# Second group of seven block products in units 1 to 7 of a SwiGLU, chains begun in five stages, gate2's modulation in the last product

## The chip, the cores and the metric

The kernel runs on one core of one Trainium2 chip. The metric is the device time of one launch in microseconds. The core's engines work side by side, each in the order of its own queue: TensorE (PE in the profile, its weight loads PEld) multiplies, VectorE (DVE) and ScalarE (ACT) do elementwise work, GpSimd (POOL) hardly anything here, and SP issues the DMA transfers.

## The reference

One layer of a decoder trunk on 256 tokens with 2048 channels, all in float32. The change touches the end of the first sub-layer's output projection (w_out) and the second sub-layer, a SwiGLU with 5632 hidden channels:

```python
mod = jax.nn.silu(c) @ w_ada[l] + b_ada[l]
shift1, scale1, gate1, shift2, scale2, gate2 = jnp.split(mod[:, None, :], N_MOD, axis=-1)
...
x = x + gate1 * mixing_sublayer(h, ...)          # ends in y @ w_out
h = rms_norm(x, norm2_gain[l]) * (1 + scale2) + shift2
gate, up = jnp.split(h @ w_ffn_in[l], 2, axis=-1)
x = x + gate2 * ((silu(gate) * up) @ w_ffn_out[l])
```

## The kernel before, in words

**Products.** The 256 tokens are two tiles of 128; the weights are the moving operand, in blocks of 512 columns, and the contraction goes in chunks of 128 rows. Each float32 operand is split into a high part that TensorE takes as it is and a low rest, and a product is three matmuls (`mm3`, L199 to L201): high times high, high times low, low times high. A chunk of a block is thus 2 x 3 matmuls of 128x512. The split of the weights goes by pairs of chunks, 128x1024: a DMA into a raw room (`raw_tile`, 512 KB), a cast on ScalarE that makes the high half (L189), a subtraction on VectorE that makes the low half (L196, in `halve`). The halves have four rooms (`whi`, `wlo`); a few pairs get tiles of their own (`spare`, `front`). The raw rooms are a list (`free_rooms`) that loads take from at the front and give back to at the end; `more_rooms` and `fewer_rooms` add tiles to it and take them out.

**Units.** The gate and up products of the SwiGLU go in 11 units of 512 hidden channels: unit i has gate block i (`pg`) and up block NFF + i (`pu`), 16 chunks each. Unit 0 is plain. From unit 1 on the first four chunks of the two blocks are a 2x2 by 2x2 block product (two token tiles, two column blocks, two pairs of chunks) done with seven block products instead of eight: `paired`. Its left sides are sums of pieces of the activations, made once (`left_sums`); its right sides are the weights' raw pieces `b11`, `b12`, `b21`, `b22` and differences of them (`t1`, `t2`, `t3` and one more), made on VectorE in `differ` into the tiles named in `places`, and each of the seven is cast and split. A product is of one token tile, so a pair of halves serves 6 matmuls there instead of 12. In the middle an intermediate sum is moved between banks (copies on ScalarE; `add` on VectorE, L1376). `paired` is a generator: the caller runs a piece of it between pieces of the up block of the unit before, so that its chain begins before it is needed. The last product (w_ffn_out, 44 chunks, four column blocks taken in two pairs) uses `paired` with two such groups (eight chunks).

The silu of the gate (L1418) and the product with the up block (L1440) give the activation, whose transposes and splits (L221, L222) are put off in `later` to a place within the following block.

**Order.** The order on each engine is fixed when the program is written out, by a scheduler that takes by priority what its own model of the engines has ready; `prio` moves a piece forward, `tc.issue_after(ins)` puts one behind `ins` on its engine. From the end of unit 0 on (`state["ordered"]`) all subtractions and differences of the weights stand on VectorE in the order in which they are written.

**gate2.** The modulation vectors are sums over 16 row blocks of w_ada, weighted by silu(c): background work (`bg`), one step per call of `tick`, which `block` calls once per pair of chunks with `state["rate"]` steps. A gate2 step is a DMA of 512 KB into a tile of the ring `ring["tags"]` and a multiply-add on VectorE (L318), 32 in all. What follows (`after`) is `rows_of`: the bias is added, and in eight rounds the sum is cast (L976), its rest taken (L977) and multiplied by ones on TensorE (L981, L982), which adds the partitions and spreads the row; each quarter is copied back (L983). One tile, T6, serves all rounds. `flush` runs what is left. Before the change gate2 goes on in units 0 to 10, and `add_out` (L1459 multiply, L1461 add) puts out each column block of the last product right after it is done.

**w_out.** The last column block of w_out has all its weights loaded ahead; the normalisation that follows and the first unit's loads are placed around it by hand (`order`, which names for each pair of chunks of unit 0 what its cast and its subtraction stand behind).

Of the kernel before, what the change touches and what calls it, by code (L numbers as in the profile page):

```python
# [17 lines left out]
P = 128  # L18
T = 256
NT = T // P  # L20
D = 2048
KC = D // P
DFF = 5632
NB = 512
# [5 lines left out]
N_DIL = 6  # L30
N_GLA = 4
SEG_SHIFT1, SEG_SCALE1, SEG_GATE1, SEG_SHIFT2, SEG_SCALE2, SEG_GATE2 = range(6)
RATE_IN, RATE_MID, RATE_FFN = 0.8, 0.6, 0.4
DEFER = 4
AHEAD = 4000
WARM = (22, 43, 10, 3)
# [4 lines left out]
NFF = 11  # L41
# [26 lines left out]
def trunk(ctx: ExitStack, tc: tile.TileContext, I, out):  # L68
# [117 lines left out]

    def halve(hi, lo, raw, high_behind=None, low_behind=None):
        with behind_it(high_behind):
            nc.scalar.copy(hi, raw)  # L189
# [1092 lines left out]
    KF = 4 * NFF  # L1282
    w_fo = I["w_ffn_out"]
    PLACES = [("A13", "A14"), ("A2", "A3")]
    LATE = {8: ("KC", "AR0"), 9: ("AR1", "A15")}

    def left_sums(tags, scratch, xh, xl):

# [9 lines left out]
        nc.vector.tensor_tensor(lo, raw, hi.bitcast(F32), op=ALU.subtract)  # L1298
        return hi, lo

    def paired(act, sums, places, src, b0, b1, k1):

        n = len(places)
        p0 = c11, c21 = [acc_bank() for _ in range(NT)]

        def halved(raw):
            hi, lo = halves_room()
# [12 lines left out]
            for r in raws:  # L1320
                give_back(r)

        with prio():
            b11, b12 = load(0, b0), load(0, b1)
            first = [halved(r) for r in b11]

        def times(ps, left, right, g, start=False):
            hi, lo = right
            for i in range(2):
# [6 lines left out]

        total = lambda q: lambda g, i: (sums[g][0][:, q, i, :], sums[g][1][:, q, i, :])
        part = lambda c, t: lambda g, i: act(4 * g + c + i, t)
        product(c11, part(0, 0), True)
# [42 lines left out]
        add(c22)  # L1382
        for q, (w, right) in enumerate(rest):
            k = 4 * n + 2 * q
            block(p0, act, None, k, k + 2, 0, w=w, go_on=True, more=True, seeded=True)
# [4 lines left out]
        block(p0, act, src, 8 * n, k1, b0, go_on=True, seeded=True)  # L1390
        yield p0, p1

    for i in range(NFF):
        if i == 0:
            pg = [acc_bank() for _ in range(NT)]
            one = turns[0]
            order = {2: (one["root"], one["spread"]), 3: (one["root"], one["spread"]), 4: (one["rows"], one["low"][0]),
                     5: (one["high"][0], one["low"][0]), 6: (one["high"][1], one["low"][1]), 7: (one["high"][2], one["low"][2])}
            w = load_weights(
                w_ff, 0, KC, 0, front=("A12", "KD", "AR0", "AR1"), spare=("A9", "A10", "A0", "A1"), behind=order  # L1400
            )
            for t in range(NT):
                block(pg, h2_at, None, 0, KC, 0, w=w, tiles=(t,), steps=steps if t == 0 else {})
            bg.append(gate2_bg())
            pu = [acc_bank() for _ in range(NT)]
        else:
            state["rate"] = (2 if i < 7 else 4) * RATE_FFN
            pg, pu = next(work)
            state["rate"] = 0.0
            if i in LATE:  # L1410
                assert not macs
                with prio():
                    act_sums.append(left_sums(LATE[i], ("A13", "A14"), *act[i - min(LATE)]))
        sgs = []
        with prio():
            for t in range(NT):
                sg = scr([P, NB])
                nc.scalar.activation(sg, pg[t], AF.Silu)  # L1418
                sgs.append(sg)
        if i == 0:  # L1420
            block(pu, h2_at, w_ff, 0, KC - 4, NFF, more=True)
            h2_sums = [left_sums(("A2", "A3"), ("A13", "A14"), h2[0][0], h2[1][0])]
            fewer_rooms("KC")
            more_rooms("A4", "A8")
            state["ordered"] = True
        else:
            block(pu, h2_at, w_ff, 4, KC - 4, NFF + i, go_on=True, more=True, seeded=True)
        if i < NFF - 1:
            work = paired(h2_at, h2_sums, [("A13", "A14")], w_ff, i + 1, NFF + i + 1, KC)
        else:  # L1430
            work = paired(act_at, act_sums, PLACES, w_fo, 0, 1, KF)
        next(work)
        block(pu, h2_at, w_ff, KC - 4, KC - 2, NFF + i, go_on=True, more=True, seeded=i > 0)
        next(work)
        block(pu, h2_at, w_ff, KC - 2, KC, NFF + i, go_on=True, seeded=i > 0)
# [12 lines left out]
    x2 = []  # L1448
    for n in range(4):
        xr = S(f"H{4 + n}", [P, NT, NB])  # L1450
        nc.sync.dma_start(xr, x2_far[:, n])
        x2.append(xr)

    LASTK, LASTC = 4, NB // 2

# [8 lines left out]

    CUT = KF - 14
    K0 = 4 * len(act_sums)
    for n in range(4):
        if n % 2 == 0:
            both = next(work)
        pss = both[n % 2]  # L1470
        if n == 3:
            fewer_rooms("H2", "H3")
            block(pss, act_at, w_fo, K0, CUT, n, more=True, go_on=True, seeded=True)
            w = load_weights(w_fo, CUT, KF, n, spare=("H2", "H3", "H4", "H5", "A2", "A3"))
# [15 lines left out]
        else:  # L1490
            if n == 1:
                block(pss, act_at, w_fo, K0, KF - 10, n, go_on=True, more=True, seeded=True)
                more_rooms("H2", "H3")
                work = paired(act_at, act_sums, PLACES, w_fo, 2, 3, KF)
                next(work)
                block(pss, act_at, w_fo, KF - 10, KF - 6, n, go_on=True, more=True, seeded=True)
                next(work)
                block(pss, act_at, w_fo, KF - 6, KF, n, go_on=True, seeded=True)
            if n == 0:
                flush()  # L1500
                gate2 = state["gate2"]
                with prio():
                    for t in range(NT):
                        add_out(n, t, pss[t])
                continue
            kept = S("H4", [P, NT, NB])
            with prio():
                for t in range(NT):
                    nc.scalar.copy(kept[:, t, :], pss[t])
            for t in range(NT):  # L1510
                add_out(n, t, kept[:, t, :])
# [47 lines left out]
```

## Time and profile before

| | |
|---|---|
| median of 3 runs | 1613.75 us (1612.1 to 1616.0) |
| the profiled execution's own time | 1612.38 us |
| its span, first to last instruction | 1610.6 us, mean granted clock 0.998 |
| DMA | 399.24 MB, mean 248 GB/s |
| units 2 to 6 | 43.5 to 43.6 us each |
| last product, 1363.62 to the last tail | 241.65 us |

The rows below are of four kinds. A row of a timeline has the start in us, the duration, the engine, the line, the operation, out<-in, the shape and in brackets how long the engine sat idle before it and what ended that. A matmul's duration is modelled and overlaps its successor's start, so two starts are compared, not the durations. A row of groups has the busy time and the mean in ns, then the idle time ahead of it. A row of windows has for each engine busy us and the number of operations, then TensorE's granted clock, the DMA engines' busy share and GB/s. A buffer's number is left out of its name: A is any of A0 to A15.

### The profile page before, as it was taken

Reading aid. Unit: us, or ns where it says so; the run is one execution under the profiler, and the core shown is the slowest. Engines: PE = TensorE matmul, PEld = TensorE weight load, DVE = VectorE, ACT = ScalarE, POOL = GpSimd, SP = SyncE. Lnnn points to the kernel's source line nnn. Section 1 sums busy time; section 2 is a strip of 40 time slices with the busy share of each in tenths; the row PEclk is TensorE's granted clock in tenths of the full one; section 3 lists DMA queues with packets and bytes.
Section 4 is the critical chain, followed back from the end, with each engine's and each line's share of the span. In section 5 each row is a group of like instructions: output and inputs, shape, how many; then the busy total and the mean of one; then the engine's idle time right before and its main releaser. Section 6 shows DMA issues by size and latency. Waiting matters only on the chain.

```text
span 1610.6 us, 20073 instructions
## 1 busy us (share of the span) xinstructions
PE 1590.7 (99%) x7273; PEld 1307.7 (81%) x7273; DVE 1241.9 (77%) x1420; ACT 851.7 (53%) x1183; POOL 5.3 (0%) x14
## 2 busy tenths in 40 slices
PE   9999999999999999999999999999999999999999
PEld 7878888788888888888887788888888888787887
DVE  6889995887888787878757788888888776856753
ACT  5654449755576444444445555555555555534542
POOL 1000000000000000000000000000000000000000
PEclk9999999999999999999999999999999999999999
DMA  9999997884776889888677577777776567765662
GB/s 335 346 330 322 330 313 222 279 264 143 253 237 217 308 301 319 309 292 310 211 210 240 176 251 259 233 247 253 246 240 191 175 194 225 260 204 177 229 179 86
DMA packets 116179, 399.24 MB, mean 248 GB/s; under 512 B 13090, under 2 KB 13896, under 8 KB 116080
## 3 DMA queue, kind: packets, MB, share of 16 engines
q1 hardware_dynamic: 115856, 397.95, 74.0%
q8 instruction: 57, 0.93, 0.2%
q14 instruction: 42, 0.34, 0.1%
q0 software_dynamic: 224, 0.01, 0.0%
HBM read 393.71 MB, written 4.19 MB: 247 GB/s over the span
## 4 chain that ended last, share of the span: by engine, by line
PE 87%; DVE 6%; issue 2%; ACT 2%; DMA 2%; ACTq 0%; DVEq 0%; SPq 0%
PE acc L201 26%; PE acc L200 26%; PE acc L199 26%; DVE wlo L196 3%; PE acc L461 1%; ACT whi L189 1%; DMA AR<-ada_rest 1%; PE misc L1104 1%; DVE ada L318 1%; PE misc L201 1%; DVE A L196 1%; PE misc L817 1%; PE misc L199 1%; PE misc L200 1%; DVE scr L1440 0%
## 5 line engine op out<-in xcount | busy, mean ns | idle before, releaser
L189 ACT CAST whi<-raw 128x1024 fp32r<-128x1024 f32 (+1 forms) x447 | 457.9, 1028 | 484.2 <-PE acc L201 364.2
L196 DVE TENSOR_TENSOR wlo<-raw,whi 128x1024 fp32r<-128x1024 f32 (+1 forms) x447 | 528.8, 1191 | 230.7 <-ACT whi L189 228.0
L200 PE MATMUL acc<-wlo,H 128*128 128x512 f32 x1476 | 576.8, 391 | 1.1 <-DVE wlo L196 1.0
L201 PE MATMUL acc<-whi,H 128*128 128x512 f32 x1476 | 576.8, 391 | 0.4 <-DVE H L480 0.4
L199 PE MATMUL acc<-whi,H 128*128 128x512 f32 x1476 | 576.4, 391 | 0.4 <-ACT H L473 0.4
L201 PEld LDWEIGHTS acc<-whi,H 128*128 128x128 f32 x1476 | 277.0, 188 | 59.0 <-DVE H L480 1.8
L200 PEld LDWEIGHTS acc<-wlo,H 128*128 128x128 f32 x1476 | 277.2, 188 | 58.0 <-DVE wlo L196 2.2
L199 PEld LDWEIGHTS acc<-whi,H 128*128 128x128 f32 x1476 | 277.1, 188 | 57.4 <-ACT H L473 1.3
L196 DVE TENSOR_TENSOR wlo<-A,whi 128x1024 fp32r<-128x1024 f32 x133 | 161.1, 1222 | 69.7 <-ACT whi L189 68.6
L189 ACT CAST whi<-A 128x1024 fp32r<-128x1024 f32 x133 | 139.8, 1053 | 131.1 <-PE acc L201 92.7
L199 PE MATMUL acc<-whi,A 128*128 128x512 f32 x332 | 130.5, 395 | 2.5 <-DVE acc L1376 1.6
L200 PE MATMUL acc<-wlo,A 128*128 128x512 f32 x332 | 129.6, 390 | 0.2 <-DVE wlo L196 0.2
L201 PE MATMUL acc<-whi,A 128*128 128x512 f32 x312 | 121.6, 390 | 0.0
L318 DVE SCALAR_TENSOR_TENSOR ada<-AR,csil,ada 128x1024 f32<-128x1024 f32 x59 | 75.1, 1279 | 6.3 <-DMA AR<-ada_rest 6.3
L199 PEld LDWEIGHTS acc<-whi,A 128*128 128x128 f32 x332 | 62.3, 188 | 19.6 <-DVE acc L1376 5.8
L200 PEld LDWEIGHTS acc<-wlo,A 128*128 128x128 f32 x332 | 62.4, 188 | 13.3 <-DVE wlo L196 0.9
L201 PEld LDWEIGHTS acc<-whi,A 128*128 128x128 f32 x312 | 58.6, 188 | 12.4
L199 PE MATMUL acc<-whi,T 128*128 128x512 f32 x120 | 46.8, 390 | 0.0
L201 PE MATMUL acc<-whi,T 128*128 128x512 f32 x120 | 46.7, 389 | 0.0
L200 PE MATMUL acc<-wlo,T 128*128 128x512 f32 x120 | 46.7, 389 | 0.0
L201 PE MATMUL acc<-whi,OS 128*128 128x512 f32 x112 | 43.6, 389 | 0.0
L517 ACT COPY A<-acc 128x512 f32<-128x512 f32 x50 | 29.0, 586 | 15.9 <-PE acc L201 14.6
(404 smaller groups left out, 1499.9 us busy)
## 6 DMA issues: line engine op xcount, KB each, us to landing
raw<-w_in SPq DMA_DIRECT2D x203, 512.0 KB, 4.9
raw<-w_ffn_in SPq DMA_DIRECT2D x122, 512.0 KB, 4.5
AR<-ada_rest SPq DMA_DIRECT2D x79, 512.0 KB, 5.0
raw<-w_ffn_out SPq DMA_DIRECT2D x53, 512.0 KB, 3.9
A<-w_ffn_in SPq DMA_DIRECT2D x52, 512.0 KB, 3.9
raw<-w_out SPq DMA_DIRECT2D x32, 512.0 KB, 3.8
KC<-ada_rest SPq DMA_DIRECT2D x30, 512.0 KB, 4.7
A<-w_ffn_out SPq DMA_DIRECT2D x29, 512.0 KB, 4.5
```

The costliest lines, as they stand in the source:

```text
L189: nc.scalar.copy(hi, raw)
L196: return nc.vector.tensor_tensor(*args, **kw)
L199: nc.tensor.matmul(ps, lh, rh, start=start, stop=False, skip_group_check=seeded)
L200: nc.tensor.matmul(ps, lh, rl, start=False, stop=False, skip_group_check=seeded)
L201: state["mm"] = nc.tensor.matmul(ps, ll, rh, start=False, stop=stop, skip_group_check=seeded)
L318: nc.vector.scalar_tensor_tensor(acc, raw, c, acc, op0=ALU.mult, op1=ALU.add)
L461: state["warm"] = nc.tensor.matmul(ps, ones_r, wide, start=True, stop=True)
L517: nc.scalar.copy(A[b][:, t, :], pss[t])
L817: nc.tensor.matmul(ps[:n, t * N_GLA + h, :].rearrange("p (s l) -> p s l", l=L), at(f, h, t)[:, :n], odd(at(f, h, t)), start=True, stop=True,)
L1104: nc.tensor.transpose(ps[:, i, :], src[:, i * P : (i + 1) * P], ident)
```

## The change

Unit i has `pairs_of(i)` groups: two in units 1 to 7, one in units 8 to 10 as before. A second set of left sums of the normalised activations is made after unit 0's gate block, in AR0, AR1. `paired` yields five times: loads and the first differences; the first product; the second product; the third difference; the rest. With `early` the differences `t2` come in the first piece. `with_stages` runs these pieces between pieces of the up block, or of the second column block in the last product. The raw rooms get OD, KD, OS1, OS2 as well until units 7 and 8. gate2's steps leave the units for the last product (ring H2, H3, H5, rate 0.65, then 2.6 for its rows); the first three column blocks of the result are kept (`keep`) and put out at the end, after `flush` at chunk 30 of the fourth, when x2 is read back too. The w_out loads of the last block are written after `flush` and `more_rooms("KC")`, and unit 0's first two casts and subtractions stand behind w_out's last (`cast3`, `split3`).

```diff
-RATE_IN, RATE_MID, RATE_FFN = 0.8, 0.6, 0.4
+RATE_IN, RATE_MID, RATE_OUT, RATE_ROWS = 0.8, 0.6, 0.65, 2.6
...
-    w = load_weights(I["w_out"], 0, KC, 3, spare=("T0", "T3", "OS0", "OS1", "OS2", "OD", "A7", "A11"))
     flush()
     more_rooms("KC")
+    w = load_weights(I["w_out"], 0, KC, 3, spare=("T0", "T3", "OS0", "OS1", "OS2", "OD", "A7", "A11"))
+    cast3, split3 = state["cast"], state["split"]
...
-    state["rate"] = RATE_FFN
-    ring["tags"] = ("AR0", "AR1", "KC")
+    state["rate"] = 0.0
...
     PLACES = [("A13", "A14"), ("A2", "A3")]
-    LATE = {8: ("KC", "AR0"), 9: ("AR1", "A15")}
+    UNIT_PLACES = [("A13", "A14"), ("KC", "A15")]
+    LATE = {9: (("KC", "AR0"), ("AR1", "A15")), 10: (("AR1", "A15"), ("A13", "A14"))}
+
+    def pairs_of(i):
+        return 2 if i < 8 else 1
...
-    def paired(act, sums, places, src, b0, b1, k1):
+    def paired(act, sums, places, src, b0, b1, k1, early):
...
+        def second_differences():
+            b22 = load(2, b1)
+            return b22, [differ(y, t, p[1]) for p, y, t in zip(places, b22, t1)]
+
+        with prio():
+            b11, b12 = load(0, b0), load(0, b1)
+            t1 = [differ(y, x, p[0]) for p, x, y in zip(places, b11, b12)]
+            if early:
+                b22, t2 = second_differences()
+        yield
+        p0 = c11, c21 = [acc_bank() for _ in range(NT)]
+        with prio():
+            first += [halved(r) for r in b11]
+            all_back(b11)
         product(c11, part(0, 0), True)
...
         yield
         side, held = misc_bank([P, NB]), scr([P, NB])
         with prio():
-            t1 = [differ(y, x, p[0]) for p, x, y in zip(places, b11, b12)]
-            all_back(b11)
             first += [halved(t) for t in t1]
-            b22 = load(2, b1)
-            t2 = [differ(y, t, p[1]) for p, y, t in zip(places, b22, t1)]
-            t3 = [differ(y, x, p[0]) for p, x, y in zip(places, b12, b22)]
-            all_back(b12)
+            if not early:
+                b22, t2 = second_differences()
         product(side, total(0), True)
...
+        yield
+        with prio():
+            t3 = [differ(y, x, p[0]) for p, x, y in zip(places, b12, b22)]
+            all_back(b12)
         yield
...
+    def in_pieces(pss, act, src, k0, k1, b, more=False):
+
+        for k in range(k0, k1, 6):
+            end = min(k + 6, k1)
+            block(pss, act, src, k, end, b, go_on=True, more=more or end < k1, seeded=True)
+            if not bg:
+                state["rate"] = RATE_ROWS
+
+    def with_stages(work, pss, act, src, k0, cuts, b):
+
+        k = k0
+        for cut in cuts:
+            if cut > k:
+                block(pss, act, src, k, cut, b, go_on=k > 0, more=cut < cuts[-1], seeded=k0 > 0)
+                k = cut
+            if cut < cuts[-1]:
+                next(work)
...
-            order = {2: (one["root"], one["spread"]), ...
+            order = {0: (cast3, split3), 1: (cast3, split3), 2: (one["root"], one["spread"]), ...
...
-            bg.append(gate2_bg())
...
         if i == 0:
-            block(pu, h2_at, w_ff, 0, KC - 4, NFF, more=True)
+            fewer_rooms("KC")
             h2_sums = [left_sums(("A2", "A3"), ("A13", "A14"), h2[0][0], h2[1][0])]
-            fewer_rooms("KC")
-            more_rooms("A4", "A8")
+            h2_sums.append(left_sums(("AR0", "AR1"), ("KC", "A15"), h2[0][1], h2[1][1]))
+            more_rooms("A4", "A8", "OD", "KD", "OS1", "OS2")
             state["ordered"] = True
+        if i in (7, 8):
+            fewer_rooms(*(("OS1", "OS2") if i == 7 else ("OD", "KD")))
+        if i < NFF - 1:
+            work = paired(h2_at, h2_sums, UNIT_PLACES[: pairs_of(i + 1)], w_ff, i + 1, NFF + i + 1, KC, True)
+            cuts = (KC - 8, KC - 4, KC - 2, KC - 2, KC)
         else:
...
+            work = paired(act_at, act_sums, PLACES, w_fo, 0, 1, KF, False)
+            cuts = (KC - 8, KC - 8, KC - 4, KC - 2, KC)
+        with_stages(work, pu, h2_at, w_ff, 0 if i == 0 else 4 * pairs_of(i), cuts, NFF + i)
...
+    ring["tags"] = ("H2", "H3", "H5")
+    bg.append(gate2_bg())
+    state["rate"] = RATE_OUT
     for n in range(4):
...
         if n == 3:
...
+            in_pieces(pss, act_at, w_fo, K0, CUT, n, more=True)
+            state["rate"] = 0.0
+            flush()
+            gate2 = state["gate2"]
+            for m, tag in ((0, "H4"), (1, "H2"), (2, "H3"), (3, "H5")):
+                x2_back(m, tag)
+            w = load_weights(w_fo, CUT, KF, n, spare=("A13", "A14", "KC", "AR0", "A2", "A3"))
+            for m in range(n):
+                for t in range(NT):
+                    add_out(m, t, kept[m][:, t, :])
...
+        if n == 1:
+            in_pieces(pss, act_at, w_fo, K0, KF - 14, n, more=True)
+            rate, state["rate"] = state["rate"], 0.0
+            work = paired(act_at, act_sums, PLACES, w_fo, 2, 3, KF, False)
+            with_stages(work, pss, act_at, w_fo, KF - 14, (KF - 12, KF - 10, KF - 6, KF - 4, KF), n)
+            state["rate"] = rate
+        keep(n, ("H6", "H7", "AR1")[n])
```

More of the change, by code (lines that the diff above doesn't have):

```diff
@@ L188, in halve @@
         with behind_it(high_behind):
-            nc.scalar.copy(hi, raw)
+            state["cast"] = nc.scalar.copy(hi, raw)
         with behind_it(low_behind):
@@ L1321, in all_back @@
                 give_back(r)
-        with prio():
-            b11, b12 = load(0, b0), load(0, b1)
-            first = [halved(r) for r in b11]
         def times(ps, left, right, g, start=False):
@@ L1338, in paired @@
         part = lambda c, t: lambda g, i: act(4 * g + c + i, t)
+        first = []
+        def second_differences():
[11 more added lines that the diff above has]
+            all_back(b11)
         product(c11, part(0, 0), True)
@@ L1384, in paired @@
             k = 4 * n + 2 * q
-            block(p0, act, None, k, k + 2, 0, w=w, go_on=True, more=True, seeded=True)
+            if q == 2 and later:
+                with tc.issue_after(state["mm"].ins), prio():
+                    later.pop()()
+            block(p0, act, None, k, k + 2, 0, w=w, go_on=True, more=k + 2 < k1, seeded=True)
+            if not bg:
+                state["rate"] = RATE_ROWS
             if q < n:
@@ L1389, in paired @@
                 times(c21, part(2, 1), right, q - n)
-        block(p0, act, src, 8 * n, k1, b0, go_on=True, seeded=True)
+        in_pieces(p0, act, src, 8 * n, k1, b0)
         yield p0, p1
+    def in_pieces(pss, act, src, k0, k1, b, more=False):
+        for k in range(k0, k1, 6):
+            end = min(k + 6, k1)
+            block(pss, act, src, k, end, b, go_on=True, more=more or end < k1, seeded=True)
+            if not bg:
+                state["rate"] = RATE_ROWS
+    def with_stages(work, pss, act, src, k0, cuts, b):
[6 more added lines that the diff above has]
+                next(work)
     for i in range(NFF):
@@ L1396, in trunk @@
             one = turns[0]
-            order = {2: (one["root"], one["spread"]), 3: (one["root"], one["spread"]), 4: (one["rows"], one["low"][0]),
+            order = {0: (cast3, split3), 1: (cast3, split3), 2: (one["root"], one["spread"]), 3: (one["root"], one["spread"]), 4: (one["rows"], one["low"][0]),
                      5: (one["high"][0], one["low"][0]), 6: (one["high"][1], one["low"][1]), 7: (one["high"][2], one["low"][2])}
@@ L1447, in trunk, with x2_back, keep @@
         act.append((hi, lo))
[L1448 to L1452, printed above, removed]
+    x2, kept = {}, {}
+    def x2_back(n, tag):
+        x2[n] = S(tag, [P, NT, NB])
+        nc.sync.dma_start(x2[n], x2_far[:, n])
+    def keep(n, tag):
+        kept[n] = S(tag, [P, NT, NB])
+        with prio():
+            for t in range(NT):
+                nc.scalar.copy(kept[n][:, t, :], both[n % 2][t])
     LASTK, LASTC = 4, NB // 2
@@ L1471, in trunk @@
         if n == 3:
-            fewer_rooms("H2", "H3")
-            block(pss, act_at, w_fo, K0, CUT, n, more=True, go_on=True, seeded=True)
-            w = load_weights(w_fo, CUT, KF, n, spare=("H2", "H3", "H4", "H5", "A2", "A3"))
+            in_pieces(pss, act_at, w_fo, K0, CUT, n, more=True)
[6 more added lines that the diff above has]
+            for m in range(n):
+                for t in range(NT):
+                    add_out(m, t, kept[m][:, t, :])
             block(pss, act_at, None, CUT, KF, 0, w=w, tiles=(0,), go_on=True, seeded=True)
@@ L1489, in trunk @@
             add_out(n, 1, side, NB - LASTC, base=NB - LASTC)
[L1490 to L1511, printed above, removed]
+            continue
+        if n == 1:
[5 more added lines that the diff above has]
+        keep(n, ("H6", "H7", "AR1")[n])
 _INS = ["x", "c", "b_ada", "norm1_gain", "norm2_gain", "sb_q_gain", "sb_k_gain", "dil_q_gain", "dil_k_gain", "w_gla_a",
```

15 lines of the change are left out of this document (1 added, 14 removed).

## The prediction, on record before the result

> **What bounds the kernel now.** I read the page's parts 1, 4 and 5 first, then cut the FFN stage into windows at the same cast of each unit, then read TensorE's rows in order of time wherever two starts lay further apart than usual. The page gives TensorE 99% of the span and the chain that ended last 87% of it; the windows name busy time and operations of TensorE, its weight loads, VectorE, ScalarE and GpSimd, then clock, DMA share and GB/s.
>
> ```profile
> PE 1590.7 (99%) x7273; PEld 1307.7 (81%) x7273; DVE 1241.9 (77%) x1420; ACT 851.7 (53%) x1183; POOL 5.3 (0%) x14
> PE 87%; DVE 6%; issue 2%; ACT 2%; DMA 2%; ACTq 0%; DVEq 0%; SPq 0%
> ```
> ```profile
> 896.00:930.53 34.53, 34.52 (x145) 27.81 (x144) 25.03 (x31) 20.26 (x26) 0.00 (x0) 0.96 0.54 168
> 1061.17:1104.73 43.56, 43.40 (x195) 35.67 (x194) 36.51 (x35) 22.94 (x26) 0.00 (x0) 1.00 0.74 254
> 1363.62:1605.27 241.65, 239.38 (x1063) 197.24 (x1062) 148.91 (x136) 108.73 (x109) 0.00 (x0) 1.00 0.62 195
> ```
>
> A unit takes 43.56 us. A busy share proves little, so look at the starts (timeline of TensorE, one unit):
>
> ```profile
> 1049.84 0.39 PE L200 MATMUL acc<-wlo,H 128*128 128x512 f32 x1
> ...
> 1058.90 0.39 PE L201 MATMUL acc<-whi,H 128*128 128x512 f32 x1
> ...
> 1065.93 0.39 PE L199 MATMUL acc<-whi,H 128*128 128x512 f32 x1
> 1066.48 0.50 PE L199 MATMUL acc<-whi,A 128*128 128x512 f32 x1 [0.16 <-DVE acc L1376]
> ```
>
> The first two rows lie 40 matmuls apart: 9.06/40 = 0.2265 us each, without a hole. The last two hold the unit's only stall, 0.55 - 0.2265 = 0.32 us, while VectorE adds a finished product into the next bank. So TensorE issues all the time, and a matmul that is left out is worth its 0.2265 us unless another engine falls behind.
>
> **The products.** Four 128-row chunks of two column blocks cost 4 x 2 x 2 x 3 = 48 matmuls plainly and 7 x 2 x 3 = 42 as a group. Units 1 to 7 get a second group: 6 fewer in each, 42 in all, 42 x 0.2265 = 9.5 us less. Units 8 to 10 and the last product keep their counts.
>
> The Trainium skill ("TensorE: Matmul & The Clock Gate", Back-to-back issue gap) gives N/2.4 + 2.5 ns, 216 ns at N = 512, for an isolated gap; by that the 42 would bring an estimated 9.1 us. The same section gives 131 ns for a sustained stream, by which they would bring 5.5 us and the case would end near 1608. The spacing here lies above both, over 40 intervals in a row, which leaves the second no chance.
>
> **Ordering of the w_out casts.** Timeline of TensorE, and of ScalarE:
>
> ```profile
> 865.57 0.39 PE L201 MATMUL acc<-OS,A 128*128 128x512 f32 x1
> 866.45 0.49 PE L199 MATMUL acc<-A,A 128*128 128x512 f32 x1 [0.49 <-ACT A L189]
> 867.71 0.50 PE L200 MATMUL acc<-A,A 128*128 128x512 f32 x1 [0.76 <-DVE A L196]
> 862.82 1.05 ACT L189 CAST A<-raw 128x1024 fp32r<-128x1024 f32 x1 [2.66 <-DMA raw<-w_ffn_in]
> 865.34 1.06 ACT L189 CAST A<-raw 128x1024 fp32r<-128x1024 f32 x1
> ```
>
> ScalarE sits 2.66 us for a piece of w_ffn_in with the last pair of w_out cast only behind it; TensorE loses 2.14 - 2 x 0.2265 = 1.7 us. The change puts the first two w_ffn_in casts behind w_out's (cast3, split3) and lends w_out the room KC. The moved halves are needed only behind w_out's second token tile, 48 matmuls or 10.9 us later, so no matmul waits anew; behind the two casts on ScalarE stand the norm's squares, which wait for w_out's end in any case: -1.7 us, or 0 if the norm chain behind it binds instead.
>
> **What pays for it.** A group needs seven halved right sides where four did: three more casts on ScalarE and three more subtractions on VectorE, and four differences. The gate2 sums (L318) leave the units. Groups of one unit, 1061.17 to 1104.73, and two rows of VectorE's timeline, 1.14 us apart at 1.22 us each:
>
> ```profile
> L318 DVE SCALAR_TENSOR_TENSOR ada<-AR,csil,ada 128x1024 f32<-128x1024 f32 x4 | 5.0, 1278 | 0.0
> L318 DVE SCALAR_TENSOR_TENSOR ada<-KC,csil,ada 128x1024 f32<-128x1024 f32 x1 | 1.3, 1279 | 0.0
> 1058.03 1.22 DVE L196 TENSOR_TENSOR wlo<-raw,whi 128x1024 fp32r<-128x1024 f32 x1
> 1059.17 1.22 DVE L196 TENSOR_TENSOR wlo<-A,whi 128x1024 fp32r<-128x1024 f32 x1
> ```
>
> VectorE per unit: 36.5 - 6.3 (five sums) + 7 x 1.14 = 38.2 us. TensorE: 43.56 - 1.36 = 42.2. ScalarE: 22.9 + 3 x 1.05 = 26.1, with the cast of the rows above. So on average all fits, VectorE at 90%. Two things decide locally. The halves have four rooms, so ScalarE's cast waits until TensorE has used the fourth one back; and subtractions and differences run strictly in the written order. In the new order the four early differences of the next unit (t1, t2) stand between the last subtraction of the paired stage and the first weights of the up block. Counted from the third of the four mixed steps there: the last room frees as that step begins, and its half is ready some 2.6 us in (cast 1.05, subtraction 1.22, waits), then come four differences, 4.6, the transposed activation's two subtractions of half the size, 1.2, and the up block's subtraction, 1.1: 9.5 us. TensorE comes for it after 36 matmuls, 8.2, and the eight transposes (43.56 - 186 x 0.2265 - 0.32 leaves 1.1 for them), and needs the low half one matmul later: 9.5. So nothing is spare there; the other halves come out early by 0.6 us or more. The old stall of 0.32 goes, since the product that covers the add is twice as long (12 matmuls, 2.7 us). What comes instead is a wait for wlo at the up block. Bounds per unit: 0, and 1.43, which is what the first front of two groups in this trace costs today (next part). I take 0.3, the old size, so the units bring 9.5 us, with ends of 7 x (1.36 + 0.32) = 11.8 and 11.8 - 7 x 1.43 = 1.8.
>
> **The two transitions into the paired last product.** Each front today is written in one piece:
>
> ```profile
> 1371.19 0.39 PE L199 MATMUL acc<-whi,KC 128*128 128x512 f32 x1
> 1372.52 0.50 PE L199 MATMUL acc<-whi,A 128*128 128x512 f32 x1 [0.94 <-ACT whi L189]
> 1383.13 0.39 PE L199 MATMUL acc<-whi,KC 128*128 128x512 f32 x1
> 1383.68 0.50 PE L200 MATMUL acc<-wlo,A 128*128 128x512 f32 x1 [0.16 <-DVE wlo L196]
> ...
> 1484.95 0.61 PE L199 MATMUL acc<-whi,OD 128*128 128x512 f32 x2
> 1486.73 0.50 PE L199 MATMUL acc<-whi,KC 128*128 128x512 f32 x1 [1.17 <-ACT whi L189]
> ```
>
> The first costs 1.33 + 0.55 less two intervals, 1.43 us, the second 1.78 less two (its first row holds two matmuls), 1.33 us, 2.8 in all. Spread over five stages most of it should go: -1.9 us, between -2.8 and 0.
>
> **Unit 0.** Here lies the first front of two groups. Its window (896.00 to 930.53) has 34.5 - 25.0 = 9.5 us of VectorE idle. Added are the second set of left sums, two subtractions and three differences (5 x 1.14 = 5.7). The sums' rows:
>
> ```profile
> 895.97 1.22 DVE L1291 TENSOR_TENSOR A<-H,H 128x1024 f32<-128x1024 f32 x1
> ...
> 898.31 0.42 DVE L1293 TENSOR_TENSOR A<-A 128x256 f32<-128x256 f32 x1
> ```
>
> One sum of 1.22, four of 0.42 and a last subtraction as large as the first make 4.1 us, so 9.8 us against 9.5. I take +1.5 us, from 0 to 4.
>
> **gate2 in the last product.** The 32 sums, 32 x 1.28 = 41 us of VectorE, go at 0.65 per pair of chunks into a stretch (1363.62 to 1605.27) with 241.7 - 148.9 = 92.7 us of VectorE idle, and 32 x 0.52 MB over some 150 us (49 pairs of chunks and the front between) add 112 GB/s to its 195, about 307, where the first unit row above shows 254 at a DMA share of 0.74. I cost both at nothing; that slack hides them, and with it gone each sum would cost its 1.28. The rest is at the end. By the rates the sums end in the last column block near chunk 20, the rows' turning is written at chunk 30, and its ones-products stand behind that chunk's matmul: 84 matmuls, 19.0 us, before TensorE's end. Eight rounds of cast, subtraction and two products follow each other through one buffer, T6. One such round:
>
> ```profile
> 1303.17 0.60 ACT L983 COPY ada<-misc 128x512 f32<-128x512 f32 x1
> 1303.65 0.43 ACT L976 CAST T<-ada 128x256 fp32r<-128x256 f32 x1
> 1305.90 0.40 ACT L976 CAST T<-ada 128x256 fp32r<-128x256 f32 x1
> 1597.04 0.69 DVE L1459 TENSOR_TENSOR scr<-ada,acc 128x512 f32<-128x512 f32 x1 [3.80 <-PE acc L201]
> 1605.27 0.75 DVE L1459 TENSOR_TENSOR scr<-ada,acc 128x256 f32<-128x256 f32 x2 [6.82 <-PE acc L201]
> ```
>
> From 1303.65 to 1305.90, 2.25 us a round, 0.48 more where a quarter is copied. Seven rounds and three copies: 17.2 us, the last products and copy take an estimated 2.0 more (the round without its cast and subtraction, and 0.60): 19.2, so the fourth quarter is there 0.2 us past TensorE's end. Today its first tile is modulated at 1597.04, nine us before the end, and the tail starts at 1605.27. Then that tile's multiply and add (2 x 0.69) push the tail back by about 2.8 us; three earlier blocks' multiplies (12 x 0.69) get in the rounds' way for some 0.5. I take +3.3 us. Low end 0 (rounds without other work in between), high end 8. On SP's queue the four reloads of x2 (2 MB) move from the stage's start to chunk 30 and six stores of 256 KB wait with their adds: 3.6 MB in 19 us, 190 GB/s, where no weights are left to load; costed at nothing, else at the one or two us that the last store would queue.
>
> **Sum.** -9.5 - 1.7 - 1.9 + 1.5 + 3.3 = -8.3 us. The profiled execution took 1612.4 us (span 1610.6), 1.4 under the median 1613.75: 1612.4 - 8.3 = 1604.1, said as 1604.
>
> **The rivals.**
> Fronts as today's: each unit's front stalls the 1.43 us of the first transition and the transitions stay as they are. Then the units bring 1.8 us, and the sum is -1.8 - 1.7 + 1.5 + 3.3 = +1.3: 1614, no change. For it: that front has the same two groups. Against it: it had six raw rooms, here ten, and six differences in a row. Chance 0.09.
>
> Slower: the lateness at the up block grows past 2 us and the clock falls with it. Its rows:
>
> ```profile
> 892.64 0.39 PE L201 MATMUL acc<-A,H 128*128 128x512 f32 x1
> 894.75 0.50 PE L199 MATMUL acc<-A,H 128*128 128x512 f32 x1 [1.72 <-ACT H L1214]
> ...
> 898.46 0.63 PE L199 MATMUL acc<-AR,H 128*128 128x512 f32 x1
> 898.89 0.49 PE L200 MATMUL acc<-AR,H 128*128 128x512 f32 x1
> ```
>
> After a hole of 1.9 us, matmuls start 0.43 apart instead of 0.2265 for some ten, 2.0 us more; the holes of 1.1 and 1.3 us above had no such sequel. Per unit 1.9 + 2.0 - 0.32 - 1.36 = +2.2, seven units +15.5, with the other terms (+1.2) 1629. It decides from about 1.8 us of lateness a unit; my working gives none. Chance 0.07.
> The Trainium skill (the same page, Part 1: The HAM clock gate) halves the clock only after an idle window of about 3.4 us; by that, holes of 1.9 us would cost themselves alone and this case would end near 1615. The trace shows half speed after a shorter hole.
>
> A late end: the rounds take 3.4 us as other work gets between; 7 x 1.15 = 8 us later, 1612 or a little less, on the edge of no change. Chance 0.07. Better than forecast (no stall in units 0 to 7, both transitions clean, the tail hidden): 11.8 + 1.7 + 2.8 = 16.3 less, 1596. Chance 0.10.
>
> **How the numbers follow.** The forecast (1598 to 1609, its bounds partly summed) has 0.67, better 0.10, as today's 0.09, late end 0.07, slower 0.07. The range 1596 to 1610 leaves out the no-change case, the slower one and a small part of the late end and of the better one, 0.2 in all. A change of 0.2%, 3.2 us, is about what this measurement can tell: faster 0.80 (half of the late end with it), same 0.13, slower 0.07.
>
> **What would show it.** TensorE 42 matmuls fewer, units 1 to 7 at 42.2 us, spacing 0.2265, VectorE 38 us busy in each; no wait at the old L1376 add but one for wlo at the up block; no ScalarE wait for w_ffn_in ahead of the last w_out cast; transitions with holes under 0.6 us each; from chunk 30 of the last block eight rounds of L976 and the first tile's multiply only after TensorE's end. I am wrong if a unit takes over 43, if DMA waits appear in the last product, or if the end lies over 8 us behind TensorE's last matmul.

## The result, and the profile after

The changed kernel takes 1597.88 us in the median (1595.6 to 1599.4, 4 runs) against 1613.8 us before: 15.9 us less, a ratio of 0.990 [0.988, 0.992]. The forecast was 1604 with a range from 1596 to 1610. The direction and its reason held; the gain was nearly twice the 8.3 us that the terms had made, and the time lies near the low end of the range.

The page of the changed kernel, part 1, and three windows as before (a unit, from its transposes to the next unit's; unit 0; the last product up to 1570):

```profile
PE 1579.5 (99%) x7231; PEld 1299.8 (81%) x7231; DVE 1298.4 (81%) x1475; ACT 877.0 (55%) x1207; POOL 5.3 (0%) x14
898.00:933.50 35.50, 35.49 (x148) 28.29 (x148) 31.85 (x39) 21.58 (x27) 0.00 (x0) 0.96 0.48 154
1079.13:1120.98 41.85, 41.85 (x190) 34.47 (x189) 38.28 (x37) 26.23 (x28) 0.00 (x0) 1.00 0.60 203
1377.90:1570.00 192.10, 192.10 (x849) 158.99 (x848) 144.60 (x128) 89.47 (x92) 0.00 (x0) 1.00 0.83 286
```

TensorE has 42 matmuls fewer, and where the windows of before had a gap between their length and TensorE's busy time, these have none: a unit is 41.85 us long and TensorE is busy for 41.85. VectorE's 38.28 us are what the prediction had added up.

The holes can be read off the waits of TensorE's matmuls, from 905 us to the end, of before and of after:

```profile
PE acc L199 <- ACT whi L189: 2.1, 2, 1.2
PE acc L199 <- DVE acc L1376: 1.6, 10, 0.2
PE acc L200 <- DVE wlo L196: 0.2, 1, 0.2
```
```profile
PE acc L199 <- DVE acc L1391: 0.5, 3, 0.2
```

The add into the next bank was waited for in ten units and is now in three, those that kept one group. Two spans cannot be compared straight, though. The chain of work shows one and the same piece, the transposes of w_out's third block, in the kernel before and in the changed one:

```profile
838.30 0.87 PE misc L1170 x8
```
```profile
841.80 0.87 PE misc L1170 x8
```

The changed kernel's profile is 3.5 us late there, and by chance: two more profiles of the changed kernel (e0 and e10 below) have TensorE begin these transposes at 838.64 and 838.35 us, where these two have 838.13 and 841.63. From there on the two take 1610.6 - 838.3 = 772.3 and 1597.2 - 841.8 = 755.4 us: the profiles differ by 16.9 us in what the change touches.

Three places that both profiles have tell where these 16.9 us lie: TensorE's first matmul behind the normalisation (at 894.75 before and 896.39 after), its wait for the add in unit 8, which has one group in both, and its last matmul (at 1606.39 and 1593.03). The half speed that the last section tells of follows the first of these places in both. The wait in unit 8, before and after:

```profile
1240.69 0.50 PE L199 MATMUL acc<-whi,A 128*128 128x512 f32 x1 [0.16 <-DVE acc L1376]
```
```profile
1230.54 0.50 PE L199 MATMUL acc<-whi,A 128*128 128x512 f32 x1 [0.16 <-DVE acc L1391]
```

Up to the normalisation the changed kernel is 1.9 us shorter, from there to unit 8 11.8 us (345.9 and 334.2), from unit 8 to the last matmul 3.2 us (365.7 and 362.5), and behind the last matmul both take 4.2 us.

### The profile page after: what moved, and what is told of

It is laid out like the page before. It is cut to its first block, busy times and chain, and to the rows that moved or that the text cites. A ratio compares the mean times of both kernels' runs of the same rounds, so it can differ in the third digit from the quotient of the medians.

```text
span 1597.2 us, 20101 instructions
## 1 busy us (share of the span) xinstructions
PE 1579.5 (99%) x7231; PEld 1299.8 (81%) x7231; DVE 1298.4 (81%) x1475; ACT 877.0 (55%) x1207; POOL 5.3 (0%) x14
## 4 chain that ended last, share of the span: by engine, by line
PE 92%; DVE 4%; DMA 2%; issue 1%; ACT 1%; POOL 0%; ACTq 0%; DVEq 0%; POOLq 0%; SPq 0%
PE acc L201 28%; PE acc L199 28%; PE acc L200 28%; DVE wlo L196 1%; DMA AR<-ada_rest 1%; PE misc L201 1%; PE misc L200 1%; PE misc L199 1%; PE misc L1104 1%; PE acc L461 1%; DVE ada L318 1%; PE misc L817 1%; ACT whi L189 1%; PE misc L454 0%; DMA H<-c 0%
## 5 line engine op out<-in xcount | busy, mean ns | idle before, releaser
L189 ACT CAST whi<-raw 128x1024 fp32r<-128x1024 f32 (+1 forms) x424 | 433.6, 1026 | 454.9 <-PE acc L201 340.2
L196 DVE TENSOR_TENSOR wlo<-raw,whi 128x1024 fp32r<-128x1024 f32 (+1 forms) x424 | 500.7, 1190 | 189.8 <-ACT whi L189 188.2
L200 PE MATMUL acc<-wlo,H 128*128 128x512 f32 x1406 | 550.7, 392 | 1.1 <-DVE wlo L196 1.0
L201 PE MATMUL acc<-whi,H 128*128 128x512 f32 x1406 | 550.7, 392 | 0.4 <-DVE H L480 0.4
L199 PE MATMUL acc<-whi,H 128*128 128x512 f32 x1406 | 549.5, 392 | 0.4 <-ACT H L473 0.4
L200 PEld LDWEIGHTS acc<-wlo,H 128*128 128x128 f32 x1406 | 264.6, 188 | 56.7 <-DVE wlo L196 3.5
L201 PEld LDWEIGHTS acc<-whi,H 128*128 128x128 f32 x1406 | 264.3, 188 | 56.2 <-DVE H L480 1.8
L199 PEld LDWEIGHTS acc<-whi,H 128*128 128x128 f32 x1406 | 264.5, 188 | 55.8 <-DVE acc L1391 1.3
L318 DVE SCALAR_TENSOR_TENSOR ada<-AR,csil,ada 128x1024 f32<-128x1024 f32 x39 | 49.7, 1280 | 7.7 <-DMA AR<-ada_rest 7.7
L318 DVE SCALAR_TENSOR_TENSOR ada<-H,csil,ada 128x1024 f32<-128x1024 f32 x30 | 37.5, 1279 | 0.1
```

What stands on the lines that cost most here:

```text
L189: state["cast"] = nc.scalar.copy(hi, raw)
L196: return nc.vector.tensor_tensor(*args, **kw)
L199: nc.tensor.matmul(ps, lh, rh, start=start, stop=False, skip_group_check=seeded)
L200: nc.tensor.matmul(ps, lh, rl, start=False, stop=False, skip_group_check=seeded)
L201: state["mm"] = nc.tensor.matmul(ps, ll, rh, start=False, stop=stop, skip_group_check=seeded)
L318: nc.vector.scalar_tensor_tensor(acc, raw, c, acc, op0=ALU.mult, op1=ALU.add)
```

## The experiments

Each ratio is to the kernel before, with its interval; each kernel is the changed one with one edit.

### The changed kernel as a reference, twice

> The changed kernel itself, so that the variants have it on the same chip. Both theories: about 16 us under the kernel before (1597.9 against 1613.8), units 1 to 7 of 41.8 us without a hole on TensorE.

> The changed kernel once more, beside the next one: 1596 to 1598.

Measured 1596.5 us, 0.990 [0.989, 0.991], and 1596.1 us, 0.990 [0.989, 0.991].

### One group in units 1 to 7

```diff
-        return 2 if i < 8 else 1
+        return 1
```

> All as in the changed kernel, but one group of block products in units 1 to 7. Theory A (TensorE's issue sets the time; what is gained is matmuls and holes): the 42 matmuls come back (+9.5) and with them the hole at the add into the next bank, 7 x 0.32 to 0.44 (+2.2 to 3.1): 1609 to 1611, units of 43.5 us. Rival B (the units got faster because gate2's sums and loads left VectorE and the DMA queues): most of the gain stays, 1598 to 1602, units of 42 us or so.

Measured 1607.9 us, 0.997 [0.996, 0.998]: 11.4 us over the changed kernel. A unit (window, from transposes to transposes):

```profile
1020.40:1063.97 43.57, 43.41 (x196) 35.66 (x195) 31.04 (x30) 22.94 (x25) 0.00 (x0) 1.00 0.60 193
```

The unit is 43.57 us long as before the change, though VectorE is busy for 31.0 us instead of 36.5 and the DMA moves 193 GB/s instead of 254. So a VectorE and DMA queues relieved of gate2 bring the units nothing by themselves; rival B falls. The group is worth 42 x 0.2265 + 7 x 0.32 = 11.8 us by the rows of before, and 11.4 was measured. From the first matmul behind the normalisation to unit 8's add this run's profile takes 346.0 us, against 334.2 in the changed kernel's: 11.8.

### Fronts in two pieces, and only the second differences late

```diff
-  ... w_ff, i + 1, NFF + i + 1, KC, True)
-            cuts = (KC - 8, KC - 4, KC - 2, KC - 2, KC)
+  ... w_ff, i + 1, NFF + i + 1, KC, False)
+            cuts = (KC - 4, KC - 4, KC - 2, KC - 2, KC)      # not in the second run
```

> The fronts of units 1 to 10 written in two pieces, as before the change, with the second differences late; groups, rooms and gate2 as in the changed kernel. If the five stages carry the two groups: holes at each front as at the first transition of the kernel before, 1.4 us in units 1 to 7, so about +10 us, 1608. If the ten raw rooms and the free VectorE are enough by themselves: units of 41.8 to 42.2 us, 1598 to 1601.

> The five stages as in the changed kernel, but the second differences of units 1 to 10 in the third stage instead of the first. The fronts in two pieces cost a hole of 0.88 us in each of seven units. If the place of the second differences makes it: the same holes, +6 us, 1602 to 1603. If the stages make it: no holes, 1597. If both do: holes of about 0.4 us, 1599 to 1600.

Measured 1602.6 us, 0.993 [0.992, 0.995], with two pieces, and 1604.9 us, 0.995 [0.994, 0.996], with five stages and the second differences late. TensorE at the front of the fourth unit, two pieces first, then five stages:

```profile
1064.04 0.39 PE L199 MATMUL acc<-whi,A 128*128 128x512 f32 x1
1065.03 0.50 PE L200 MATMUL acc<-wlo,H 128*128 128x512 f32 x1 [0.60 <-DVE wlo L196]
```
```profile
1062.28 0.39 PE L199 MATMUL acc<-whi,A 128*128 128x512 f32 x1
1063.27 0.50 PE L200 MATMUL acc<-wlo,H 128*128 128x512 f32 x1 [0.60 <-DVE wlo L196]
```

The same hole to a hundredth, 0.99 - 0.2265 = 0.76 us and a slow start behind it, in each of seven units. VectorE's rows just ahead of it, in the run with five stages:

```profile
1057.46 1.22 DVE L196 TENSOR_TENSOR A<-A,A 128x1024 f32<-128x1024 f32 x1
1058.59 1.22 DVE L196 TENSOR_TENSOR A<-raw,KC 128x1024 f32<-128x1024 f32 x1
1059.73 1.22 DVE L196 TENSOR_TENSOR A<-A,raw 128x1024 f32<-128x1024 f32 x1
1060.86 1.22 DVE L196 TENSOR_TENSOR KC<-raw,A 128x1024 f32<-128x1024 f32 x1
1062.00 1.22 DVE L196 TENSOR_TENSOR wlo<-raw,whi 128x1024 fp32r<-128x1024 f32 x1
```

Four differences in a row stand ahead of the low half that TensorE waits for; it comes at 1062.00 + 1.22 and the matmul starts at 1063.27. That the pieces are spread over five stages does not matter as long as those four lie there. What carries the two groups is that the second differences lie in the first piece, before the up block's weights, and by the times that is worth 6 to 9 us, or 0.9 to 1.3 a unit; by the traces it is 1.0 a unit, as the next front lies 42.84 us behind the one shown in both runs, where a unit of the changed kernel takes 41.85. Whether two pieces would do with the second differences early was not run, nor what the four added raw rooms are worth. Here the waits of the changed kernel's weight loads, units 1 to 7:

```profile
PEld acc L199 <- DVE acc L1391: 1.3, 7, 0.2
PEld acc L200 <- DVE wlo L196: 1.1, 6, 0.2
```

Both waits are still there, in seven and in six of the seven units, 0.2 us long, and TensorE's matmuls show none of it there. The front fits with little to spare.

### gate2 back in the units

```diff
-    state["rate"] = 0.0
+    state["rate"] = 0.7
+    ring["tags"] = ("T3", "T4", "T5")
...
+            bg.append(gate2_bg())             # after unit 0's gate block
...
-    ring["tags"] = ("H2", "H3", "H5")
-    bg.append(gate2_bg())
```

> gate2's 32 sums back in units 0 to 6 (ring T3, T4, T5, rate 0.7), nothing of it in the last product; two groups as in the changed kernel. If VectorE's room decides: 38.3 us busy plus 5.5 sums of 1.19 us make 44.8 us against TensorE's 41.8, so these units go to 44 to 45 us, +13 to +19 us in six or seven units, 1611 to 1616. If VectorE's idle time can take them (its 38.3 us hold waits that the sums could fill only in part): units of 42 to 43 us, 1599 to 1605. If gate2 in the units cost nothing, 1598.

Measured 1625.2 us, 1.007 [1.006, 1.008]. All three expectations missed the mechanism. Window of a unit, window of the unit where it broke, and TensorE there:

```profile
993.87:1035.71 41.84, 41.84 (x189) 34.41 (x188) 41.78 (x40) 25.96 (x29) 0.00 (x0) 1.00 0.69 240
1161.20:1203.00 41.80, 18.36 (x78) 14.49 (x77) 35.45 (x34) 10.46 (x13) 0.00 (x0) 0.74 0.71 246
1177.82 0.39 PE L201 MATMUL acc<-whi,H 128*128 128x512 f32 x1
1201.65 0.80 PE L199 MATMUL acc<-whi,H 128*128 128x512 f32 x1 [23.44 <-ACT scr L1454]
```

The units did not get slower: VectorE is busy for 41.78 of 41.84 us, and TensorE does not notice. But only three sums a unit got in, since halves and differences go first; the others piled up, and the last eight ran in the hole shown. In the sixth unit gate2's rows, written by then, took the scratch buffers for the bias and waited for the last sum, and the next silu waited for a scratch buffer: 23.4 us in one piece. So the load is not paid as a small price in each unit, it is put off until something in the written order has to wait for it.

A second run asked for no more than VectorE's room (0.37 a pair of chunks, ring T5 and OS0; from unit 8 on 0.8, ring AR0 and AR1):

> gate2's 32 sums in units 0 to 9 again, but no faster than VectorE's idle time of 3.5 us a unit lets them: 0.37 per pair of chunks, 3 sums a unit, through unit 7 (ring T5, OS0), then 0.8 (ring AR0, AR1); none in the last product. If VectorE's room is the only limit: units 1 to 7 stay at 41.8 to 42.0 us with VectorE busy throughout, nothing piles up ahead of a silu, and the whole is at the changed kernel's time, 1595 to 1599. If a VectorE without any idle time makes the low halves late: holes of 0.3 to 1 us a unit, 1599 to 1604.

Measured 1602.7 us, 0.993 [0.992, 0.995], 6.6 us over the changed kernel of the same batch. A unit, and TensorE at unit 9's front:

```profile
1034.30:1076.30 42.00, 42.00 (x190) 34.45 (x189) 41.41 (x40) 26.23 (x28) 0.00 (x0) 1.00 0.70 234
1270.96 0.39 PE L199 MATMUL acc<-whi,H 128*128 128x512 f32 x1
1273.17 0.50 PE L199 MATMUL acc<-whi,A 128*128 128x512 f32 x1 [1.82 <-DVE acc L1392]
1274.24 0.63 PE L200 MATMUL acc<-wlo,A 128*128 128x512 f32 x1
1274.67 0.63 PE L201 MATMUL acc<-whi,A 128*128 128x512 f32 x1
```

Three sums a unit cost 0.15 us each unit. The rest had to go into units 8 and 9, and there the add into the next bank came 2 us late. Against e10's profile of the changed kernel this one takes 0.8 us more from the normalisation to unit 8's add, and 6.0 us more from there to TensorE's last matmul. So in this arrangement the two groups and all of gate2 do not fit into the units together; the loss lies where the leftover goes, and another place for it could lose less. That gate2 moved is thus worth about 6 us against this one arrangement, though it brings nothing by itself.

### w_out's casts ordered as before

```diff
-            order = {0: (cast3, split3), 1: (cast3, split3), 2: ...
+            order = {2: ...                   # and the loads ahead of flush() again
```

> The changed kernel with w_out's loads and unit 0's first two casts ordered as before the change. Theory A: the two holes of 0.65 and 1.03 us ahead of w_out's last pair come back, +1.7 us and no more. Rival: the normalisation behind it sets that stretch (TensorE waits 1.9 us for its first high half anyway), and the time is the same within 0.5 us.

Measured 1598.8 us, 0.990 [0.988, 0.992]; an effect of this size is not told by the times. TensorE shows it, this run first, then the changed kernel at the same pair:

```profile
870.43 0.39 PE L201 MATMUL acc<-OS,A 128*128 128x512 f32 x1
871.18 0.50 PE L199 MATMUL acc<-A,A 128*128 128x512 f32 x1 [0.36 <-ACT A L189]
872.44 0.50 PE L200 MATMUL acc<-A,A 128*128 128x512 f32 x1 [0.76 <-DVE A L196]
```
```profile
869.07 0.39 PE L201 MATMUL acc<-OS,A 128*128 128x512 f32 x1
869.30 0.39 PE L199 MATMUL acc<-A,A 128*128 128x512 f32 x1
869.52 0.39 PE L200 MATMUL acc<-A,A 128*128 128x512 f32 x1
```

The holes are back, 2.01 - 2 x 0.2265 = 1.56 us, and gone without it. The hole of 1.9 us behind it, where the norm's first half is waited for, is there in both, so it only moved along: from the first row shown to the matmul behind that hole this run takes 29.0 us (870.43 to 899.44) and the changed kernel 27.3 (869.07 to 896.39), so the 1.6 us are kept.

### The last product's fronts in two pieces

```diff
-            cuts = (KC - 8, KC - 8, KC - 4, KC - 2, KC)
+            cuts = (KC - 4, KC - 4, KC - 2, KC - 2, KC)
...
-  (KF - 12, KF - 10, KF - 6, KF - 4, KF)
+  (KF - 10, KF - 10, KF - 6, KF - 6, KF)
```

> The changed kernel with the two fronts of the last product in two pieces as before the change. Theory A: holes of 1.4 and 1.3 us come back, +2.8 us. Rival: those holes came from VectorE and the loads in the crowd of that place (silu products, left sums, x2's loads), which has changed; then under 1 us.

Measured 1598.0 us, 0.990 [0.988, 0.992]. One hole came back, at the first front:

```profile
1355.74 0.39 PE L199 MATMUL acc<-whi,KC 128*128 128x512 f32 x1
1356.73 0.50 PE L200 MATMUL acc<-wlo,H 128*128 128x512 f32 x1 [0.60 <-DVE wlo L196]
```

That is 0.76 us, and with slower starts behind it and at the second front the run takes 276.7 us from unit 10's add (1315.00) to TensorE's last matmul (1591.72), against 275.4 in the changed kernel (1317.65 to 1593.03). So the pieces are worth 1.3 of the 2.8 us that both fronts cost before, about halfway between theory A and its rival. These two pieces are not quite the old ones, as the first differences stand ahead of the first product here; what of the 1.5 us left belongs to that and what to the crowd (left sums a unit later, x2's loads gone) was not taken apart.

### gate2's rows closer to the end

```diff
-    CUT = KF - 14
+    CUT = KF - 8
```

> gate2's rows begin at chunk 36 of the last column block instead of chunk 30, so 48 matmuls, 10.9 us, before TensorE's end instead of 84. In the changed kernel the rows take 18.3 us from their first product to the last copy and end 4.0 us before TensorE. If that chain is as long wherever it starts, the last quarter comes 18.3 - 10.9 = 7.4 us less what the first round's wait of 5 us behind four subtractions shrinks, and the end moves by 3 to 8 us. If the rows have their slack from elsewhere (they can start earlier on ScalarE and VectorE), the end does not move.

Measured 1596.5 us, 0.989 [0.987, 0.990]; the end did not move. The rows hardly moved either. Their first product lies 19.2 us ahead of TensorE's last matmul instead of 21.9, where the edit was meant to take off 8.2, and their last copy ends 2.9 us ahead of it instead of 3.6. The likely reason, which was not tested, is that with six chunks more ahead of `flush` the rate of 2.6 runs longer. The edit did not do what it was meant to, and where the rows begin to cost stays open.

### Two groups in units 8 and 9 too

```diff
-        return 2 if i < 8 else 1
+        return 2 if i < 10 else 1
...
-  ... w_ff, i + 1, NFF + i + 1, KC, True)
+  ... w_ff, i + 1, NFF + i + 1, KC, i < 8)
```

> Two groups in units 8 and 9 as well (unit 9 with its second differences late, as six raw rooms hold no more). Theory A: 12 matmuls fewer and two holes at the add: 2 x (1.36 + 0.32 to 0.44) = -3.4 to -3.6 us, the fastest of all, about 1594.5. Rival: with eight and then six raw rooms and the left sums of the last product in unit 9, loads or VectorE come late: a hole of 1 to 2 us in each of the two units, no gain.

> Two groups in units 8 and 9 as well, once more beside the changed kernel: 12 matmuls and two holes less, one hole of 0.9 us at unit 9's front more: 2 x 1.68 - 0.88 = 2.5 us under it, 1594 to 1595.5. No gain if what its first run showed was the chip's.

Measured 1594.9 us, 0.988 [0.986, 0.989], and 1595.1 us, 0.989 [0.988, 0.990], beside 0.990 [0.989, 0.991] of the changed kernel twice. TensorE, unit 9's front:

```profile
1267.82 0.39 PE L199 MATMUL acc<-whi,A 128*128 128x512 f32 x1
1268.81 0.50 PE L200 MATMUL acc<-wlo,H 128*128 128x512 f32 x1 [0.60 <-DVE wlo L196]
```

It is the fastest version both times and has the one hole expected, but it is 0.9 us under the changed kernel beside it and 1.6 under the earlier one, inside the intervals. It beats the kernel before; over the changed one the times do not settle it, but the traces do: from the first matmul behind the normalisation to unit 10's add the first of these runs takes 417.5 us (896.06 to 1313.51), and e0 and e10 of the changed kernel take 419.5. That is 2.0 us less, where 12 matmuls and two holes fewer and one new hole had made 2.5, and behind that point all three take 275.4 us to TensorE's last matmul.

## Why the prediction was right, and what was mis-sized

The steps held in their signs except two, and each size can be set beside its measurement.

**The units (-9.5 forecast).** A matmul was worth its 0.2265 us. The stall kept at the old size was the term that failed: it measured none, and the second group brought 11.4 us by the times and 11.8 by the traces (one group against two). The working for the up block, 9.5 us of VectorE against 9.5 of TensorE, was right to the tenth (the low half ends at 1087.22 + 1.22 us and TensorE's matmul with it starts at 1088.56); VectorE in the changed kernel, with the turned activation's split, the four differences and the up block's first two subtractions:

```profile
1081.48 1.28 DVE L222 TENSOR_TENSOR A<-misc,A 128x512 fp32r<-128x512 f32 x2
1082.68 1.22 DVE L196 TENSOR_TENSOR A<-OD,A 128x1024 f32<-128x1024 f32 x1
...
1086.08 1.22 DVE L196 TENSOR_TENSOR A<-OS,KC 128x1024 f32<-128x1024 f32 x1
1087.22 2.35 DVE L196 TENSOR_TENSOR wlo<-raw,whi 128x1024 fp32r<-128x1024 f32 x2
```

I then added 0.3 us for safety where the sum had said zero. The far bound, 1.43 us a unit, was the cost of the wrong order of differences: with that order it measured 1.0 us by the traces.

**w_out (-1.7).** By the traces -1.6 to -1.9.

**The transitions (-1.9).** All 2.8 us went. The reason given, the stages, is shown for 1.3 of it only.

**Unit 0 (+1.5).** It measured nothing: VectorE is busy for 31.85 of 35.5 us and TensorE for 35.49. The term put 9.8 us into that window; by 31.85 - 25.03 = 6.8 us of more, over a window one us longer that holds more matmuls (148 against 145), part of that work fell outside it.

**The end (+3.3).** The sum set 19.2 us of the rows' chain against 19.0 us of TensorE. ScalarE's rows of two rounds and a copy, VectorE's of the fourth block's first tile and of the tail, and TensorE's first product of the rows and its last matmul:

```profile
1578.36 0.41 ACT L976 CAST T<-ada 128x256 fp32r<-128x256 f32 x1
1580.03 0.41 ACT L976 CAST T<-ada 128x256 fp32r<-128x256 f32 x1 [1.27 <-PE misc L982]
1582.02 0.41 ACT L976 CAST T<-ada 128x256 fp32r<-128x256 f32 x1
1589.49 0.69 DVE L1498 TENSOR_TENSOR scr<-ada,acc 128x512 f32<-128x512 f32 x1 [0.49 <-ACT ada L983]
1591.91 0.75 DVE L1498 TENSOR_TENSOR scr<-ada,acc 128x256 f32<-128x256 f32 x2 [1.01 <-PE acc L201]
1571.15 0.28 PE L981 MATMUL misc<-T,ones_r 128*128 128x256 f32 x1
1593.03 0.28 PE L201 MATMUL acc<-A,H 128*128 128x256 f32 x1
```

The size of a round was wrong: it takes 1.67 us, 1.99 with a copy, where 2.25 and 2.73 were taken from one round of before that had a split of 1.2 us (L222) ahead of its subtraction. But the second round stood behind four subtractions of the weights and took 6.1 us (1572.30 to 1578.36), which gave most of that back: from 1571.15 to 1589.49 are 18.3 us against the 19.2. The larger error was TensorE's stretch, 21.9 us from the rows' first product to the last matmul, where 84 matmuls had made 19.0: the rows' own sixteen products lie among them and were left out. So the fourth quarter was ready 3.5 us ahead of the last matmul's start, its first tile is multiplied ahead of TensorE's end and not behind it as expected, and the tail waits for TensorE as it did.

**Costed at nothing**, and rightly: gate2's sums in the last product. Its window to 1570 shows 192.10 us of TensorE in 192.10, at a DMA share of 0.83 and 286 GB/s (307 was worked out). Waits for transfers, which the prediction named as a sign of being wrong, did appear: ScalarE waits three times for pieces of w_ffn_out, 1.1 to 1.4 us each, but none of it reaches TensorE.

The terms that were off were all off in the cautious direction. Forecast were -9.5, -1.7, -1.9, +1.5 and +3.3, or -8.3; by the traces they are -11.8, about -1.7, -2.8, 0 and 0, or -16.3, of the 16.9 between the two profiles; the rest was not taken apart. That is the case that the prediction called better than forecast, 16.3 less and 1596, at one chance in ten. So the mechanism was right, that TensorE's issue sets the time and a relieved VectorE brings nothing by itself, while the number 1604 rests on margins that were not needed, and the range held the result by 2 us. The slower rival needed about 1.8 us of lateness at the up block; the wrong order of the differences made a hole of 0.76.

## What to carry to other kernels

Where TensorE's starts lie at one fixed distance, a matmul is worth that distance and a relieved VectorE nothing, so count matmuls and holes, and let the other engines' sums only say whether they still fit. When an engine that feeds it fills up, ask which of its queue's instructions stand ahead of the one waited for: two differences a unit, moved by a few places, decided 1.0 us a unit, while work of low priority filled nearly all of the same engine's time for 0.15 us a unit. Put-off work is not free, though: look for the buffer or the result that somebody in the written order will wait for.

## What the runs showed of the hardware that was not expected

The hole of 2.1 us ahead of unit 0, where the norm's first half is waited for, is in all fourteen profiles, 2.10 to 2.12 us from start to start, but half speed follows it in five of them only. Of the changed kernel's three profiles one has it; the granted clock is 0.83 there over 892 to 902 us, and 1.00 over 889 to 897 in e0. The rows are those of e10, where the starts behind the hole soon lie 0.23 apart:

```profile
890.99 0.39 PE L201 MATMUL acc<-A,H 128*128 128x512 f32 x1
893.09 0.50 PE L199 MATMUL acc<-A,H 128*128 128x512 f32 x1 [1.72 <-ACT H L1214]
...
894.62 0.40 PE L201 MATMUL acc<-A,H 128*128 128x512 f32 x1
894.86 0.39 PE L199 MATMUL acc<-AR,H 128*128 128x512 f32 x1
```

Where half speed follows, seven or eight matmuls start 0.43 us apart, and the twelve matmuls behind the hole take 1.3 to 1.6 us longer than where it does not. In the run with gate2 spread over the units the hole of 2.2 us at unit 9's front, shown there, brought it too, while its hole at the norm did not. So a hole of 2 us throttles at times and at times not. The Trainium skill ("TensorE: Matmul & The Clock Gate", Part 1: The HAM clock gate) describes a free-running window of about 3.4 us, which fits that the same hole is treated differently from run to run; that an idle time well under 3.4 us can be enough is what these rows add.
